# Back-to-back layer 0 projections, an on-chip transpose, LN2 behind the last adds, and pooling in pieces

## The chip, the cores and the metric

The kernel runs on the 8 cores of one Trainium2 chip (trn2). Each core computes one batch element of 8, with its own weights in its own transfers; nothing is exchanged between cores. The metric is the time of the slowest core, in microseconds (us) on the device, as the median of several executions.

In fast runs all eight cores show about the same mean granted TensorE clock (about 0.97 in the kernel before). In slow runs the cores of one die or of both show a lower clock and the time is 3 to 20% longer. Slow runs are left out everywhere below. A core here is a pipeline of TensorE (PE in the profile), VectorE (DVE), ScalarE (ACT), GpSimd (POOL) and SyncE (SP); POOL issues the DMA transfers that cast float32 to bfloat16 on the way (queue q0), SP the plain ones (queue q1).

## The reference, cut to what matters

```python
D_MODEL, BATCH, SEQ, DEPTH = 1024, 8, 2048, 4      # D_FF = 2816
for i in range(DEPTH):
    if i % 2 == 0:   # layers 0 and 2
        h = x @ w_in + b_in                        # 1024 -> 2048
        h = val * sigmoid(gate)                    # the two halves of h
        h = causal depthwise conv(h, width 31) + b_dw
        mix = silu(layer_norm(h)) @ w_out + b_out
    else:            # layers 1 and 3
        # trailing means over 2, 4, 8 and 16 tokens, one window per 256 channels,
        # minus x, then a 256x256 map per group
        mix = multiscale_pool(x, ...)
    x = layer_norm(alpha * x + mix)                # LN1
    x = layer_norm(alpha * x + swiglu(x))          # LN2
```

Most of the arithmetic is the SwiGLU feed-forward network (FFN). Softer spots are the serial chains: projection, convolution, LayerNorm, output projection, LN1, and only then the FFN.

## The kernel before

A core's 2048 tokens are two blocks of 1024, and a block is 8 "rows" of 128 tokens. The program is one list of operations with declared reads and writes; a list scheduler places them at build time, and each engine runs its own list in order. While the FFN of one block runs on TensorE, the mixer of the next stage (the other block, or the next layer) runs beside it. Only the first mixer, of block 0 in layer 0, has no FFN to hide behind.

The start loads x twice for each block, as it is and transposed on the host, and loads both blocks and the first FFN weights as soon as their buffers are free:

```python
def load_block(b):
    for i in range(4):
        plload(xTb[b][:, 2 * i:2 * i + 2]..., xt_d[b, 2 * i:2 * i + 2]..., ...)   # casting queue
    for q in range(P):
        spload(xtok[b][:, q, :], x_d[...][:, q, :], [("X", b, q)], ...)           # plain queue

load_block(0)
load_consts()
mixer(0, 0)
load_block(1)
for i, (L, b) in enumerate(stages):
    if i + 1 < len(stages):
        mixer(b2, L2)
    S.cls = 1
    ffn(b, L)
    S.cls = 0
```

The input projection takes its weights in 8 chunks through two small buffers; each chunk's result goes to a scratch tensor in memory (`scr`) and comes back in another layout as the input U of the convolution:

```python
for c in range(8):
    wo = YX_O + (c % 2) * 4 * KB
    plload(ar16(wo, 2048), win_d[L][c], ...)       # 512 KB written per chunk
    for h in range(2):                             # half the rows
        # 2 x 8 matmuls of 512 columns, two ACT evictions, one DVE product
    # store to scr[c], load scr[c] into U
for cg in range(16):
    # DVE builds masks (0.82 us each, 2 per group), 20 small matmuls, DVE adds bias
```

At the end of each FFN the sum is added row by row from PSUM and LN2 follows after every fourth row, in the same VectorE list:

```python
for q in range(P):
    # 14 or 16 matmuls for row q into one of two pairs of PSUM banks
    S.op("dve", ... xs = xs + ps ...)              # frees the pair of banks
    if last:
        ln_stats(0, xs, xk, q)
        if q % 4 == 3:
            ln_rstd(0, q - 3, q + 1)
            for qq in range(q - 3, q + 1):
                ln_apply(0, ...)                   # 2 x 1.28 us per row
```

The pooling mixer adds whole shifted copies of x: one VectorE addition covers up to 20 rows of 256 channels (5120 columns, 5.48 us in the profile). For block 0 two more passes over 2048 columns make the mean and subtract x, 2.28 us each; for block 1 one pass does both.

Of the kernel before, what the change touches and what calls it, by code (L numbers as in the profile page):

```python
# [14 lines left out]
DEPTH = 4  # L15
# [34 lines left out]
class Sched:  # L50
# [3 lines left out]
    DMA_RATE = 280e3  # L54
# [3 lines left out]
    def __init__(self):  # L58
        self.prog = []
        self.ops = {e: [] for e in self.ENGS}  # L60
        self.cnt = {e: 0 for e in self.ENGS}
        self.dcnt = {}
        self.last_w = {}
        self.readers = {}
        self.seen = {e: {} for e in self.ENGS}
        self.semkeys = set(self.ENGS)
        self.eng_free = {e: 0.0 for e in self.ENGS}
        self.dma_free = 0.0
        self.fin = {}
        self.cls = 0  # L70

    def op(self, eng, fn, reads=(), writes=(), dma=None, dur=0.5, nbytes=0, pri=0):
        self.prog.append((eng, fn, tuple(reads), tuple(writes), dma, dur, nbytes, pri + self.cls))

    def schedule(self):
        prog = self.prog
        n = len(prog)
        last_w, readers = {}, {}
        preds = [None] * n
        succs = [[] for _ in range(n)]  # L80
        for i, (eng, fn, reads, writes, dma, dur, nb, pri) in enumerate(prog):
            ps = set()
            for r in reads:
                w = last_w.get(r)
                if w is not None:
                    ps.add(w)
            for k in writes:
                w = last_w.get(k)
                if w is not None:
                    ps.add(w)  # L90
                ps.update(readers.get(k, ()))
            for r in reads:
                readers.setdefault(r, []).append(i)
            for k in writes:
                last_w[k] = i
                readers[k] = []
            ps.discard(i)
            preds[i] = ps
            for p in ps:
                succs[p].append(i)  # L100
        left = [len(p) for p in preds]
        avail = [0.0] * n
        ready = {i for i in range(n) if left[i] == 0}
        while ready:
# [14 lines left out]
            f = self.commit(prog[i], st)  # L119
# [10 lines left out]
    def commit(self, desc, start):  # L130
        eng, fn, reads, writes, dma, dur, nbytes, pri = desc
# [3 lines left out]
        else:  # L135
            self.eng_free[eng] = start + dur
            t0 = max(start + dur, self.dma_free)
            self.dma_free = t0 + nbytes / self.DMA_RATE
            fin = self.dma_free + self.DMA_LAT
        idx = len(self.ops[eng])  # L140
        deps = []
        for r in reads:
            if r in self.last_w:
                deps.append((self.last_w[r], True))
        for w in writes:
            if w in self.last_w:
                deps.append((self.last_w[w], False))
            deps.extend((t, False) for t in self.readers.get(w, ()))
        need = {}
        for (sk, val, peng, pdma), raw in deps:  # L150
            if (not pdma) and peng == eng and dma is None:
                if eng == "pe":
                    continue
# [15 lines left out]
        for r in reads:  # L169
            self.readers.setdefault(r, []).append(tick)  # L170
        for w in writes:
            self.last_w[w] = tick
            self.readers[w] = []
# [3 lines left out]
    def final_wait(self, eng, keys):  # L177
        need = {}
        for k in keys:
            t = self.last_w.get(k)  # L180
            cands = list(self.readers.get(k, ()))
            if t is not None:
                cands.append(t)
            for (sk, val, *_r) in cands:
                if need.get(sk, 0) < val:
                    need[sk] = val
# [3 lines left out]
def build():  # L190
# [6 lines left out]
    xt_d = dram("xt", [NBLK, P, 128, 8 * 128])  # L197
# [17 lines left out]
    with es:  # L215
# [56 lines left out]
        def spload(out, src, keys, sem, nbytes, reads=()):  # L272
            S.op("sp", lambda e: e.dma_start(out=out, in_=src), reads=reads, writes=keys,
                 dma=sem, dur=0.1, nbytes=nbytes)

        def plload(out, src, keys, sem, nbytes, pri=0):
            S.op("pool", lambda e: e.dma_start(out=out, in_=src), writes=keys, dma=sem,  # L277
                 dur=0.9, nbytes=nbytes, pri=pri)
# [5 lines left out]
        def ln_stats(st, src, keys, q):  # L284
            for eh in range(2):
                S.op("dve", lambda e, eh=eh: e.bn_stats(  # L286
                    out=stt[:, st, q, eh, :], in_=src[:, eh * 512:(eh + 1) * 512]),
                    reads=keys, writes=[("STT", st, q, eh)], dur=t_dve(512))
# [32 lines left out]
        def x_to_xT(b, q, slot, bank):  # L321
            S.op("act", lambda e: e.activation(out=xb[:, slot, :], in_=xtok[b][:, q, :], func=AF.Copy),  # L322
                 reads=[("X", b, q)], writes=[("XB", slot)], dur=t_act(1024))
# [17 lines left out]
        def conv_mixer(b, L):  # L341
            U_O, US_O, WC_O, WT_O, YX_O, BD_O = 0, 33 * 512, 41 * 512, 51 * 512, 61 * 512, LN1O
# [6 lines left out]
            spload(ar32(BD_O, 1024), vec_d[L, 0], ark(BD_O, 4096), "d_bd", 512e3)  # L349
            plload(ar16(WC_O, NG * ND * P), wcol_d[L], ark(WC_O, NG * ND * P * 2), "d_wc", 1.3e6)  # L350
# [6 lines left out]
            for c in range(8):  # L357
                ws = c % 2
                wo = YX_O + ws * 4 * KB
                plload(ar16(wo, 2048), win_d[L][c], ark(wo, 4096), f"d_win{ws}", 1e6)  # L360
                w = ar16(wo, 2048)
                us = c % 2
                uo = US_O + us * 2 * KB
                for h in range(2):
                    b0 = PS_M[ring("pm", 3)]
                    b1 = PS_M[ring("pm", 3)]
                    vo = YX_O + 8 * KB + ring("vb", 2) * 2 * KB
                    to = YX_O + 12 * KB + ring("th", 2) * 2 * KB

                    def mm(e, off, bank, w=w, h=h):  # L370
                        ins = None
                        for k in range(8):
                            ins = e.matmul(ps[:, bank, :], w[:, off + k * 128: off + (k + 1) * 128],
                                           xTb[b][:, 4 * h:4 * h + 4, k, :],
                                           start=(k == 0), stop=(k == 7))
                        return ins
                    rk = ark(wo, 4096) + xtk(b, range(4 * h, 4 * h + 4))
                    S.op("pe", lambda e, mm=mm, b0=b0: mm(e, 0, b0), reads=rk, writes=[("PS", b0)],
                         dur=8 * PE512)
                    S.op("pe", lambda e, mm=mm, b1=b1: mm(e, 1024, b1), reads=rk, writes=[("PS", b1)],  # L380
                         dur=8 * PE512)
                    S.op("act", lambda e, b0=b0, vo=vo, c=c: e.activation(  # L382
                        out=ar32(vo, 512), in_=ps[:, b0, :], func=AF.Identity,
                        bias=hbt[L][:, c:c + 1], scale=0.5),
                        reads=[("PS", b0), ("HB", L)], writes=ark(vo, 2048), dur=t_act(512) + 0.09)
                    S.op("act", lambda e, b1=b1, to=to, c=c: e.activation(  # L386
                        out=ar32(to, 512), in_=ps[:, b1, :], func=AF.Tanh,
                        bias=hbt[L][:, 8 + c:9 + c], scale=0.5),
                        reads=[("PS", b1), ("HB", L)], writes=ark(to, 2048), dur=t_act(512) + 0.09)
                    S.op("dve", lambda e, vo=vo, to=to, uo=uo, h=h: e.scalar_tensor_tensor(  # L390
# [484 lines left out]
```

## Time and profile before

| | before |
|---|---|
| median of fast runs | 2587.11 us (four runs, 2586.47 to 2589.12) |
| profiled execution, slowest core | 2589.9 us |
| TensorE busy | 2364.6 us, 91% |
| VectorE busy | 1612.7 us, 62% |

First the page of the kernel before: busy times, then four rows that cut the span into 40 equal slices of 65 us (digits are tenths), then the chain of work that ended last.

```profile
PE 2364.6 (91%) x12672; PEld 1146.4 (44%) x12672; DVE 1612.7 (62%) x1950; ACT 652.4 (25%) x852; POOL 229.5 (9%) x434
...
PE   2273899999999999999999999999999999999996
...
PEclk9597899999999999999999999999999999999998
DMA  9851274653764466546465276625653565347431
...
PE 78%; DVE 9%; DMA 5%; issue 5%; another core or an unknown queue 2%; POOL 1%; ACT 0%; DVEq 0%; SPq 0%; POOLq 0%; ACTq 0%
```

TensorE is full from the sixth slice on. The first five, up to 325 us, are poor, and DMA is 80% full or more in just the first two. The timeline of TensorE for the first 135 us of before (start, duration, operation, what it wrote and read, how many instructions, and in brackets the idle time ahead and what ended it) shows why:

```profile
44.41 16.87 PE L746 MATMUL ps<-sb_xT,sb_arena 128*128 128x512 bf16 x64 [44.41 <-DMA sb_arena<-win]
113.95 21.43 PE L746 MATMUL ps<-sb_xT,sb_arena 128*128 128x512 bf16 x88 [52.66 <-DMA sb_arena<-win]
```

The first matmul waits 44.4 us for the first weights, and after 64 matmuls, two chunks, TensorE stands 52.7 us for the third. In stretches of 20 us (columns: busy time of PE, PEld, DVE, ACT, POOL, then granted clock, DMA share, GB/s) the DMA engines are full with other data meanwhile, the clock falls to half, and around 210 us VectorE is full while TensorE has nothing else to do:

```profile
80.00:100.00 20.00, 0.00 (x0) 0.00 (x0) 0.00 (x0) 0.00 (x0) 0.00 (x0) 0.50 1.01 176
...
200.00:220.00 20.00, 2.60 (x12) 1.35 (x13) 20.00 (x35) 4.83 (x6) 0.00 (x0) 0.51 0.28 76
```

The first FFN matmul comes at 264.56 us:

```profile
264.56 3.59 PE L746 MATMUL ps<-sb_xT,sb_wgu 128*128 128x512 bf16 x8 [1.11 <-ACT sb_xT L318]
```

The second loss is at each FFN's end. The groups of TensorE instructions of before (count, busy us, mean ns of one, and idle ahead of them by releaser) give its sum, and the timeline its form:

```profile
L746 PE MATMUL ps<-sb_wd,sb_hT 128*128 128x512 bf16 x2816 | 637.3, 386 | 36.8 <-DVE sb_xtok L689 36.8
```

```profile
629.51 3.19 PE L746 MATMUL ps<-sb_wd,sb_hT 128*128 128x512 bf16 x14 [1.37 <-DVE sb_xtok L689]
636.74 4.88 PE L746 MATMUL ps<-sb_wd,sb_hT 128*128 128x512 bf16 x14 [4.03 <-DVE sb_xtok L689]
```

The matmuls of a row cannot start until the addition two rows earlier (line 689) has emptied their banks, and that addition stood behind this VectorE run of four LN2 operations:

```profile
630.10 4.86 DVE L306 SCALAR_TENSOR_TENSOR sb_xtok<-sb_xtok,sb_rs,sb_ln2p 128x1024 f32<-128x1024 f32 x4
```

After the wait the clock is down (0.72 on average from 636 to 642 us, 1.00 in the 6 us before) and 14 matmuls take 4.88 us, not 3.19.

### The profile page before, as it was taken

To read this page: it belongs to the slowest core of one execution; us is meant where nothing else is said; L and a number is where in the kernel's file an instruction comes from. 1 tells how busy PE (TensorE), PEld (TensorE's weight loads), DVE (VectorE), ACT (ScalarE), POOL (GpSimd) and SP (SyncE) were. 2 spreads that over 40 slices of the span, in tenths; PEclk is the share of its full clock that TensorE was granted. 3 is DMA by queue.
4 is the path that set the end of the run, shared out by engine and by line. 5 is a ranking of instruction groups with operands and counts; after the bars stand their busy time and mean duration, and the time that the engine had idled before them with its cause. 6 is when DMAs were issued, how large, how long until landed. Compare 5 with 4: busy or idle time off the path is not lost.

```text
span 2589.9 us, 31036 instructions; the slowest of 8 cores (2575.8 to 2589.9 us)
## 1 busy us (share of the span) xinstructions
PE 2364.6 (91%) x12672; PEld 1146.4 (44%) x12672; DVE 1612.7 (62%) x1950; ACT 652.4 (25%) x852; POOL 229.5 (9%) x434
## 2 busy tenths in 40 slices
PE   2273899999999999999999999999999999999996
PEld 1141345444445445544544445544445544544442
DVE  0059426868796778561686634776797679754226
ACT  1023430332113313333033342233102311322110
POOL 2000000100010001100011010100010011001100
PEclk9597899999999999999999999999999999999998
DMA  9851274653764466546465276625653565347431
GB/s 210 158 103 33 44 138 78 110 94 59 137 123 73 70 138 99 96 78 126 78 106 88 57 130 117 108 62 98 121 100 73 95 130 90 50 77 159 80 63 65
DMA packets 128566, 253.33 MB, mean 98 GB/s; under 512 B 43494, under 2 KB 56740, under 8 KB 127908
## 3 DMA queue, kind: packets, MB, share of 16 engines
q0 software_dynamic: 62944, 170.49, 42.2%
q1 hardware_dynamic: 65480, 80.85, 10.5%
q8 instruction: 101, 1.65, 0.3%
q14 instruction: 41, 0.34, 0.1%
HBM read 391.35 MB, written 16.91 MB: 158 GB/s over the span
## 4 chain that ended last, share of the span: by engine, by line
PE 78%; DVE 9%; DMA 5%; issue 5%; another core or an unknown queue 2%; POOL 1%; ACT 0%; DVEq 0%; SPq 0%; POOLq 0%; ACTq 0%
PE ps L746 76%; DMA sb_arena<-win 3%; PE ps L752 2%; DVE sb_xtok L303 2%; DVE sb_xtok L306 2%; DVE sb_stt L286 2%; DVE sb_xtok L689 1%; DMA sb_arena<-sb_xtok 1%; DMA sb_wgu<-wgu 1%; DVE sb_arena L430 0%; POOL sb_wd L277 0%; DVE sb_arena L458 0%; DMA scr_0<-sb_arena 0%; DVE sb_mv L289 0%
## 5 line engine op out<-in xcount | busy, mean ns | idle before, releaser
L746 PE MATMUL ps<-sb_xT,sb_wgu 128*128 128x512 bf16 x5632 | 1247.9, 380 | 6.3 <-DVE sb_hT L658 3.8
L746 PEld LDWEIGHTS ps<-sb_xT,sb_wgu 128*128 128x128 bf16 x5632 | 545.6, 98 | 641.6 <-DVE sb_hT L658 7.1
L746 PE MATMUL ps<-sb_wd,sb_hT 128*128 128x512 bf16 x2816 | 637.3, 386 | 36.8 <-DVE sb_xtok L689 36.8
L658 DVE TENSOR_TENSOR sb_hT<-ps,sb_sgt 128x512 bf16<-128x512 f32 x352 | 240.9, 689 | 431.2 <-PE ps L746 427.4
L654 ACT ACTIVATE sb_sgt<-ps 128x512 f32<-128x512 f32 x352 | 208.5, 597 | 1021.4 <-PE ps L746 915.6
L746 PEld LDWEIGHTS ps<-sb_wd,sb_hT 128*128 128x128 bf16 x2816 | 276.0, 99 | 372.7 <-DVE sb_xtok L689 44.2
L746 PE MATMUL ps<-sb_xT,sb_arena 128*128 128x512 bf16 x1024 | 232.2, 387 | 103.8 <-DMA sb_arena<-win 101.6
L689 DVE TENSOR_TENSOR sb_xtok<-sb_xtok,ps 128x1024 f32<-128x1024 f32 x128 | 155.8, 1217 | 94.7 <-PE ps L746 94.7
L746 PEld LDWEIGHTS ps<-sb_xT,sb_arena 128*128 128x128 bf16 x1024 | 101.0, 99 | 231.6 <-issue 111.7
L390 DVE SCALAR_TENSOR_TENSOR sb_arena<-sb_arena 128x512 bf16<-128x512 f32 x64 | 44.2, 691 | 254.3 <-ACT sb_arena L386 236.8
L277 POOL DMA_DIRECT2D sb_wgu<-wgu x176 | 93.7, 532 | 1121.6 <-PE ps L746 1093.4
L746 PE MATMUL ps<-sb_arena 128*128 128x128 bf16 (+2 forms) x1792 | 178.1, 252 | 13.2 <-DVE sb_arena L430 13.1
L286 DVE BATCH_NORM_STATS2 sb_stt<-sb_xtok 128x6 f32<-128x512 f32 x256 | 166.7, 683 | 0.8
L746 PEld LDWEIGHTS ps<-sb_arena 128*128 128x128 bf16 x1792 | 128.4, 99 | 70.0 <-DVE sb_arena L430 17.0
L277 POOL DMA_DIRECT2D sb_wd<-wd x176 | 93.8, 555 | 569.1 <-PE ps L746 503.3
L318 ACT ACTIVATE sb_xT<-ps 128x1024 bf16<-128x1024 bf16 x96 | 98.1, 1022 | 143.3 <-PE ps L752 143.1
L430 DVE TENSOR_TENSOR sb_arena<-sb_maskb,sb_arena 128x1280 bf16<-128x1280 bf16 x128 | 99.6, 816 | 43.5 <-DMA sb_arena<-wcol 33.9
L685 DVE SCALAR_TENSOR_TENSOR sb_xtok<-sb_xtok,ps 128x1024 f32<-128x1024 f32 x64 | 77.8, 1215 | 47.6 <-PE ps L746 47.5
L322 ACT ACTIVATE sb_xb<-sb_xtok 128x1024 bf16<-128x1024 f32 x80 | 84.2, 1053 | 45.6 <-DVE sb_xtok L306 45.6
L382 ACT ACTIVATE sb_arena<-ps,sb_hb 128x512 f32<-128x512 f32 x64 | 44.0, 687 | 153.8 <-PE ps L746 153.1
L303 DVE SCALAR_TENSOR_TENSOR sb_xtok<-sb_xtok,sb_mv,sb_arena 128x1024 f32<-128x1024 f32 x64 | 81.7, 1276 | 0.8
L577 DVE TENSOR_TENSOR sb_arena<-sb_arena 128x2048 f32<-128x2048 f32 (+3 forms) x24 | 80.2, 3340 | 0.0
(58 smaller groups left out, 1279.5 us busy)
## 6 DMA issues: line engine op xcount, KB each, us to landing
sb_wgu<-wgu POOLq DMA_DIRECT2D x176, 512.0 KB, 6.3
sb_wd<-wd POOLq DMA_DIRECT2D x176, 256.0 KB, 9.9
sb_arena<-win POOLq DMA_DIRECT2D x32, 512.0 KB, 7.6
sb_arena<-vec SPq DMA_DIRECT2D x24, 512.0 KB, 4.7
sb_xtok<-x SPq DMA_DIRECT2D x16, 512.0 KB, 33.1
sb_arena<-lnp SPq DMA_DIRECT2D x16, 512.0 KB, 5.5
sb_ln2p<-lnp SPq DMA_DIRECT2D x16, 512.0 KB, 9.8
sb_arena<-wout POOLq DMA_DIRECT2D x32, 256.0 KB, 4.0
```

The lines of the kernel that those rows point to most:

```text
L277: S.op("pool", lambda e: e.dma_start(out=out, in_=src), writes=keys, dma=sem, dur=0.9, nbytes=nbytes, pri=pri)
L286: S.op("dve", lambda e, eh=eh: e.bn_stats(out=stt[:, st, q, eh, :], in_=src[:, eh * 512:(eh + 1) * 512]), reads=keys, writes=[("STT", st, ...
L303: S.op("dve", lambda e: e.scalar_tensor_tensor(out=src, in0=src, scalar=mv[:, st, q, 0:1], in1=g, op0=ALU.subtract, op1=ALU.mult), reads=k ...
L318: S.op("act", lambda e: e.activation(out=dst, in_=psb[bank], func=AF.Copy), reads=[("PS", bank)], writes=dkeys, dur=t_act(1024))
L322: S.op("act", lambda e: e.activation(out=xb[:, slot, :], in_=xtok[b][:, q, :], func=AF.Copy), reads=[("X", b, q)], writes=[("XB", slot)], ...
L430: S.op("dve", lambda e, wt=wt, g0=g0: e.tensor_tensor(out=ar16(wt, 1280).rearrange("p (a c q) -> p a c q", a=10, q=P), in0=maskb[:].rearra ...
L577: S.op("dve", lambda e, B=B, nn=nn, step=step: e.tensor_tensor(out=B[:, 0:nn, :], in0=B[:, step:step + nn, :], in1=B[:, 0:nn, :], op=ALU.add),
L654: S.op("act", lambda e, h=h, bank=bank: e.activation(out=sgt[:, h, :], in_=ps[:, bank, :], func=AF.Silu), reads=[("PS", bank)], writes=[(" ...
L658: S.op("dve", lambda e, h=h, bank=bank, jj=jj: e.tensor_tensor(out=hT[:, jj, h * 512:(h + 1) * 512], in0=ps[:, bank, :], in1=sgt[:, h, :], ...
L685: S.op("dve", lambda e, xs=xs, pv=pv: e.scalar_tensor_tensor(out=xs, in0=xs, scalar=ALPHA, in1=pv, op0=ALU.mult, op1=ALU.add), reads=xk + ...
L689: S.op("dve", lambda e, xs=xs, pv=pv: e.tensor_tensor(out=xs, in0=xs, in1=pv, op=ALU.add), reads=xk + [("PS", bp), ("PS", bp + 1)], writes ...
L746: r = self.e.matmul(*a, **k)
```

## The change

The intent, in four parts:

1. **Front.** Host-transposed x is dropped; x is cast and transposed on the chip. The 8 weight chunks of layer 0 stay resident in buffers that the FFN does not need yet, so that the projections of *both* blocks use one load and block 1's projections can fill holes of block 0's chain. Block 1's x waits for block 0's scratch stores, and the early FFN weights cannot load because their buffers hold projection weights and convolution results.
2. **LN2 behind the last adds.** All eight additions of the last group come first; LN2 follows under the next stage's FFN. Only the very last FFN keeps LN2 between, in ranges of 4, 2, 1 and 1 rows.
3. **Pooling in pieces** of at most 1024 columns, one full pass less for block 0, and halo copies that may run side by side.
4. **The last FFN** takes its groups in the reverse order, so that its last group is the longest.

The diff also changes the build-time scheduler (its model of the DMA queues, and writes to one buffer that may run side by side) and lets block 0's first convolution start group by group.

The core of the diff (cut):

```diff
+        def win_home(L, c):
+            ...
+            if c < 4:
+                return (hTf[:, c * 2048:(c + 1) * 2048], [("HT", j, h) ...])
+            i = c - 4
+            return wdf[:, i * 2048:(i + 1) * 2048], [("WD", 2 * i), ("WD", 2 * i + 1)]
...
+        def first_xT(b, qs):
+            for q in qs:
+                i = 1 if b else q % 2
+                x_to_xT(b, q, i, 6 + i, cast="act" if b else "dve")
...
+        def load_x(b, qs):
             for q in range(P):
+                hold = [("SCR", 0, 0, q)] if b else []
                 spload(xtok[b][:, q, :], ..., hold)
...
-        load_block(0)
         load_consts()
+        load_x(0, range(P))
+        for c in range(8):
+            load_win(0, c)
+            if c == 1:
+                load_dw(0)
+        first_xT(0, range(P))
         mixer(0, 0)
-        load_block(1)
+        load_x(1, range(P))
+        S.cls = 1
+        first_xT(1, range(P))
+        for c in range(8):
+            p1_chunk(1, 0, c)
+        S.cls = 0
...
                     if last:
                         ln_stats(0, xs, xk, q)
-                        if q % 4 == 3:
-                            ln_rstd(0, q - 3, q + 1)
-                            for qq in range(q - 3, q + 1):
-                                ln_apply(0, ...)
+                        if end and q + 1 in (4, 6, 7, 8):
+                            ln2_tail(b, L, {4: 0, 6: 4, 7: 6, 8: 7}[q + 1], q + 1)
+                if last and not end:
+                    S.cls = 0
+                    ln2_tail(b, L, 0, 4)
+                    ln2_tail(b, L, 4, 8)
...
+        def pieces(n, m=4):
+            k = (n + m - 1) // m
+            return [(n * i // k, n * (i + 1) // k) for i in range(k)]
...
-                if nh > 1:
-                    S.op("dve", ... out=B[:, 0:nh - 1, :], in0=B[:, 1:nh, :], in1=B[:, 0:nh - 1, :] ...)
+                for a, z in pieces(nh - 1):
+                    S.op("dve", ... out=B[:, a:z, :], in0=B[:, a + 1:z + 1, :], in1=B[:, a:z, :] ...)
```

## The prediction

> **What bounds the kernel now.** TensorE is busy 91% of a 2589.9 us span (busy table). A warm 512-column matmul takes 0.2157 us (16 in 3.45 us in the timeline), a 128-column transpose about 0.055, a convolution matmul 0.065, a 256-column one 0.11. For 9984 + 1152 + 1280 + 256 of them I estimate 2332 us of pure matmul time. About 258 us are lost; the windows show where:
> - First 360 us: about 172 us of warm work, 187 us lost. The first matmul waits until 44.4 us for weights; after 64 matmuls it stands 52.7 us for weight chunk 2 (chain of waits). DMA is full until about 110 us: both blocks' x, transposed x and FFN weights, wanted only at 265 us, are ahead of those chunks. From 160 to 265 us VectorE is nearly full (convolution masks, LayerNorm) and TensorE has nothing else to do. The clock falls to 0.5 to 0.7 in the holes.
> - Seven FFN ends: 1.37 + 4.03 us idle, because two PSUM adds stand behind LN2 applies (one run of 4.86 us). The matmuls after are cold (14 take 4.7 us, not 3.05). About 7.2 us each, 50 in all.
> - The end: 15.7 us after the last matmul, about 7 before it.
> Between, TensorE has no gap worth naming, apart from 3 us behind a 5.48 us pooling add.
>
> **What the change does.**
> 1. Front. The transposed x goes away, the second block's x waits for the first block's scratch stores, FFN weights cannot be loaded early (their buffers hold other things). The first projections wait for block 0's x (4.2 MB, plain queue) and weight chunk 0. Before, about 5.7 MB plain and 3.3 MB casting transfers landed in 42 us; at these shares row 7 of x lands at about 33 us, chunk 0 at 12, and later chunks keep ahead. Projections begin at about 20 us on half the rows and run freely from 36. Added: 16 groups of 8 transposes, 7 us of TensorE; 8 casts on VectorE, 8 on ScalarE.
> The second block's projections (55 us of TensorE) fill the VectorE-bound stretch of block 0. Work before the first FFN matmul is then about 165 us, FFN start at 205 to 215 us (265 before, with the 55 us still to do). Loss in the front about 48 us instead of 187: gain 139, less 7 for transposes.
> 2. LN2 behind the last adds: an add and its statistics take 2.7 us of VectorE, one per 3.03 us of matmuls, so the adds keep up. The LayerNorm, about 20 us, moves under the next FFN, where VectorE has room; mixers end 23 us or more before they are needed. Gain about 45 of 50.
> 3. Pooling in pieces: about 3 us.
> 4. Last FFN with groups reversed: about 3 us; its tail stays VectorE-bound.
>
> Sum: 2332 + 7 + 48 + 20 (end) + 3 = 2410 us.
>
> **Prediction.** 2410 us, range 2385 to 2445. Faster by over 2%: 0.97; within 2%: 0.02; slower: 0.01.
>
> **What would show it.** First projection at 18 to 25 us, no wait for projection weights over 5 us; DMA not full at 100 us; first FFN matmul at 195 to 220 us; no wait on last FFN adds over 1 us except in the last FFN; TensorE idle behind VectorE near zero after 360 us.
>
> **What would make it wrong.** Scratch round trips stalling the in-order TensorE queue; late FFN weights; convolution and LayerNorm of block 0 stretched by block 1's work on VectorE; LN2 applies delaying FFN products in the next stage.

## The result, and the profile after

| | before | after |
|---|---|---|
| median | 2587.11 us | 2444.92 us of the three fast runs (2444.61 to 2445.84) |
| ratio of fast runs | 1 | 0.945, 95% interval 0.9431 to 0.9468 |
| profiled execution, slowest core | 2589.9 us | 2442.9 us |
| TensorE busy | 91% | 96% |
| VectorE busy | 62% | 67% |

A ratio is the mean time of one kernel's fast runs over the mean of the other's of the same rounds, so it is not quite the ratio of the medians quoted beside it. With the one slow run counted, the median of the four runs after is 2445.38 us. The output was correct. The change is faster by 142 us. The prediction was 2410 with a range of 2385 to 2445: the class is right, the number about 35 us too low, at the very edge of the range.

The page of after, the rows that answer to those above:

```profile
PE 2348.7 (96%) x12800; PEld 1152.6 (47%) x12800; DVE 1631.6 (67%) x2056; ACT 676.3 (28%) x878; POOL 219.1 (9%) x418
...
PE   4997899999999999999999999999999999999996
...
PEclk9998899999999999999999999999999999999998
DMA  8564655446744664565735464743754384428531
...
PE 89%; DMA 5%; DVE 3%; SPq 1%; issue 1%; ACT 1%; DVEq 0%; ACTq 0%
```

The first five slices are fuller (4 9 9 7 8 against 2 2 7 3 8), and VectorE's share of the chain falls from 9% to 3%. The timeline of TensorE after shows the new start:

```profile
11.04 1.03 PE L840 MATMUL ps<-sb_identb,sb_xb 128*128 128x128 bf16 x8 [11.04 <-DVE sb_xb L320]
...
28.93 3.60 PE L834 MATMUL ps<-sb_xT,sb_hT 128*128 128x512 bf16 x8 [1.12 <-ACT sb_xT L312]
...
46.91 1.03 PE L840 MATMUL ps<-sb_identb,sb_xb 128*128 128x128 bf16 x8 [3.79 <-DVE sb_xb L320]
47.74 22.24 PE L834 MATMUL ps<-sb_xT,sb_hT 128*128 128x512 bf16 x96
```

The 52.7 us wait for weights is gone. What remains is x: its rows land one by one until 46 us (the last cast, on VectorE, waits for its row), and free projections begin at 47.74, not at 36 as predicted:

```profile
46.16 0.69 DVE L320 CAST sb_xb<-sb_xtok 128x1024 bf16<-128x1024 f32 x1 [3.53 <-DMA sb_xtok<-x]
```

In front of the first FFN, and again in front of the second half of its rows, the same timeline has two holes that the prediction did not cost:

```profile
194.71 3.62 PE L834 MATMUL ps<-sb_arena,sb_wgu 128*128 128x512 bf16 x16
207.56 1.03 PE L840 MATMUL ps<-sb_identb,sb_xb 128*128 128x128 bf16 x8 [9.24 <-ACT sb_xb L317]
210.66 1.03 PE L840 MATMUL ps<-sb_identb,sb_xb 128*128 128x128 bf16 x8 [2.06 <-ACT sb_xb L317]
...
219.08 3.57 PE L834 MATMUL ps<-sb_xT,sb_wgu 128*128 128x512 bf16 x8 [1.21 <-ACT sb_xT L312]
...
247.71 3.62 PE L834 MATMUL ps<-sb_arena 128*128 128x512 bf16 x16
255.95 2.32 PE L834 MATMUL ps<-sb_arena 128*128 128x128 bf16 x20 [4.62 <-DMA sb_arena<-scr_1]
...
268.96 3.55 PE L834 MATMUL ps<-sb_xT,sb_wgu 128*128 128x512 bf16 x8 [1.12 <-ACT sb_xT L312]
```

From the output projection of row 3 (ending at 198.3) to the first FFN matmul (219.08), TensorE does four groups of 8 transposes. Each row costs 3.1 us there: a ScalarE cast, 8 transposes, a ScalarE copy, in a line; in the code all rows go through one cast buffer and one bank. The first 8 us of the hole are row 3's LN1 and the last applies on VectorE: the first cast starts at 206.45. Block 1's projections, meant as the filler, were used up just before. The same happens for rows 4 to 7 from 251.3 to 268.96. The wait of 4.62 us for scr_1 in there is not what holds it up: the first cast of that group could not start before 256.92, when VectorE's LN1 let go of its row.

LN2's waits are gone. The group of after that answers to the 36.8 us of before:

```profile
L834 PE MATMUL ps<-sb_wd,sb_hT 128*128 128x512 bf16 x2816 | 618.4, 379 | 0.9 <-DVE sb_hT L737 0.9
```

36.8 us of waiting and 18.9 us of cold matmuls (637.3 less 618.4) have become 0.9. The sum of waits of TensorE from 360 to 2424 us (us in total, times, longest), before and after:

```profile
PE ps L746 <- DVE sb_xtok L689: 31.4, 14, 4.0
PE ps L752 <- ACT sb_xb L322: 4.1, 2, 2.1
PE ps L746 <- DVE sb_hT L658: 3.8, 4, 2.5
...
```

```profile
PE ps L834 <- DVE sb_hT L737: 8.3, 6, 3.1
```

So 8.3 us of waiting for FFN products (line 737) are left, against 3.8 before. The timeline of VectorE after at one of them shows what stands in front:

```profile
585.42 2.22 DVE L620 TENSOR_TENSOR sb_arena<-sb_arena 128x768 f32<-128x768 f32 x2 [6.84 <-DMA sb_arena<-sb_xtok]
...
588.85 0.68 DVE L737 TENSOR_TENSOR sb_hT<-ps,sb_sgt 128x512 bf16<-128x512 f32 x1
```

VectorE runs in order. It stands 6.84 us at a pooling addition that waits for its halo copy, while an FFN product that could run stands behind it. The two longest waits of TensorE (2.37 us at 834.81 and 3.12 us at 1760.62) have the same form, behind halo waits of 8.52 and 9.28 us.

A tally of after, from these lines, against a pure matmul time of 2324 us (an estimate: 9984 matmuls of 512 columns at 0.2157, 1280 transposes and 1280 convolution matmuls at 0.0555 each, since 20 of the latter take 1.11 us back to back, 256 of 256 columns at 0.11):

| loss in after | us | read from |
|---|---|---|
| until 47.74 us | 41 | 47.7 less 7.0 of matmuls done |
| 48 to 194 us | 4 | small gaps at 109 to 119, cold matmuls |
| 198.3 to 219.08, and cold after | 22 | 20.7 less 1.8 of transposes, plus 2.6 |
| 251.3 to 268.96, and cold after | 17 | 17.6 less 2.9 of work, plus 2 |
| pooling waits, and cold after | 12 | 8.3, plus 1.7 twice |
| after the last matmul (2423.8) | 19 | 2442.9 less 2423.8 |
| sum | 115 | 2442.9 less 2324 is 119 |

The front of after thus loses 84 us, where 48 were predicted.

### The profile page after: what moved, and what is told of

It reads as the page before. It is cut to its first block, busy times and chain, and to the rows that moved or that the text cites. A ratio compares the mean times of both kernels' runs of the same rounds, so it can differ in the third digit from the quotient of the medians.

```text
span 2442.9 us, 31400 instructions; the slowest of 8 cores (2435.8 to 2442.9 us)
## 1 busy us (share of the span) xinstructions
PE 2348.7 (96%) x12800; PEld 1152.6 (47%) x12800; DVE 1631.6 (67%) x2056; ACT 676.3 (28%) x878; POOL 219.1 (9%) x418
## 4 chain that ended last, share of the span: by engine, by line
PE 89%; DMA 5%; DVE 3%; SPq 1%; issue 1%; ACT 1%; DVEq 0%; ACTq 0%
PE ps L834 86%; PE ps L840 3%; DMA sb_arena<-sb_xtok 2%; DMA sb_arena<-vec 2%; DVE sb_xtok L300 1%; SPq L615 1%; DVE sb_xtok L297 1%; ACT sb_xb L317 0%; DVE sb_stt L280 0%; DVE sb_hT L737 0%; DVE sb_arena L636 0%; SPq L267 0%; DVE sb_arena L620 0%; DVE sb_xtok L769 0%; DMA sb_arena<-scr_0 0%
## 5 line engine op out<-in xcount | busy, mean ns | idle before, releaser
L834 PE MATMUL ps<-sb_wd,sb_hT 128*128 128x512 bf16 x2816 | 618.4, 379 | 0.9 <-DVE sb_hT L737 0.9
L312 ACT ACTIVATE sb_xT<-ps 128x1024 bf16<-128x1024 bf16 x108 | 110.4, 1022 | 174.8 <-PE ps L840 174.8
L840 PE MATMUL ps<-sb_identb,sb_xb 128*128 128x128 bf16 x768 | 64.4, 232 | 57.5 <-DVE sb_xb L320 33.8
L834 PE MATMUL ps<-sb_xT,sb_arena 128*128 128x512 bf16 x512 | 112.8, 379 | 0.0
L462 DVE TENSOR_TENSOR sb_arena<-sb_maskb,sb_arena 128x1280 bf16<-128x1280 bf16 x128 | 100.8, 816 | 17.4 <-PE ps L834 17.4
L317 ACT ACTIVATE sb_xb<-sb_xtok 128x1024 bf16<-128x1024 f32 x88 | 92.7, 1053 | 58.5 <-DVE sb_xtok L300 55.3
L840 PEld LDWEIGHTS ps<-sb_identb,sb_xb 128*128 128x128 bf16 x768 | 53.8, 104 | 79.2 <-DVE sb_xb L320 35.5
L636 DVE TENSOR_TENSOR sb_arena<-sb_arena 128x1024 f32<-128x1024 f32 x72 | 86.2, 1213 | 0.0
L408 DVE SCALAR_TENSOR_TENSOR sb_arena<-sb_arena 128x512 bf16<-128x512 f32 x32 | 22.1, 692 | 91.0 <-ACT sb_arena L404 83.3
```

Of the source, the lines that this page charges most:

```text
L312: S.op("act", lambda e: e.activation(out=dst, in_=psb[bank], func=AF.Copy), reads=[("PS", bank)], writes=dkeys, dur=t_act(1024))
L317: S.op("act", lambda e: e.activation(out=xb[:, slot, :], in_=xtok[b][:, q, :], func=AF.Copy), reads=[("X", b, q)], writes=[("XB", slot)], ...
L462: S.op("dve", lambda e, wt=wt, g0=g0: e.tensor_tensor(out=ar16(wt, 1280).rearrange("p (a c q) -> p a c q", a=10, q=P), in0=maskb[:].rearra ...
L636: S.op("dve", lambda e, B=B, step=step, a=a, z=z: e.tensor_tensor(out=B[:, a:z, :], in0=B[:, a + step:z + step, :], in1=B[:, a:z, :], op=A ...
L834: r = self.e.matmul(*a, **k)
L840: r = self.e.transpose(*a, **k)
```

## The experiments

My theory after the result: the front is right in mechanism and short by some 36 us, because x lands late (it shares the DMA engines with the weights) and because the LN1 chain of one row after another has no filler left; LN2 paid in full; pooling in pieces matters more than I had said. The rivals were that the front's gain is mere transfer order (then holding back loads in the kernel before gives most of it), that LN2's gain comes alone, and that the late x is a share of bytes and not of packets.

The runs were made on four chips. The kernel before took means of 2584.2, 2590.7, 2588.5 and 2587.6 us on them, so differences of a few us are read as "saved against before on the same chip". After itself saves 142.3 so (0.945, interval about plus or minus 5 us).

### a_ln2_back: LN2 back among the last adds

```diff
-                if last and not end:
-                    S.cls = 0
-                    ln2_tail(b, L, 0, 4)
-                    ln2_tail(b, L, 4, 8)
+                        if not end and q % 4 == 3:
+                            ln2_tail(b, L, q - 3, q + 1)
```

> The changed kernel with one part undone: the seven inner LN2 tails stand again among the last adds, as before the change. Theory (adds behind LN2 applies): the gaps before the last adds come back, 1.4 + 4.0 us each plus cold matmuls, so 45 to 55 us slower than the changed kernel, about 2495 us. Rival (the gain at the FFN ends is small because the LayerNorm only moves and is paid again in the next FFN): under 25 us slower.

Measured: 2493.83 and 2494.61 us in its two fast runs of four, 49 us above after (saved 90.0 against before, so 52 less than after). The group of its last FFN matmuls:

```profile
L832 PE MATMUL ps<-sb_wd,sb_hT 128*128 128x512 bf16 x2816 | 637.5, 386 | 31.5 <-DVE sb_xtok L769 31.5
```

31.5 of waiting and 19.1 of cold matmuls make 50.6 us, less after's 0.9. In the new kernel LN2's place is worth about 50 us, as expected.

### e_before_ln2: the kernel before with that one part alone

```diff
-                        if q % 4 == 3:
-                            ln_rstd(0, q - 3, q + 1)
-                            for qq in range(q - 3, q + 1):
+                    if last and q == P - 1:
+                        end = (L, b) == (DEPTH - 1, NBLK - 1)
+                        S.cls = 1 if end else 0
+                        for hq in (3, 7):
+                            ln_rstd(0, hq - 3, hq + 1)
+                            for qq in range(hq - 3, hq + 1):
```

> The kernel before with one part of the change alone: LN2 behind the last adds in every FFN, pooling whole, front as before. If the parts simply add, it gains the 49 us that undoing this part cost in the changed kernel: about 2538 us. Theory (LN2 pushed into the next stage delays the pooling inputs, and whole pooling adds then hold up FFN products; in the changed kernel without pieces such waits came to 19 us instead of 8): the gaps at the FFN ends are gone, but waits behind VectorE in the pooling layers rise from 4 to 12 us or more, and the time is 2543 to 2556 us.

Measured: one fast run, 2565.36 us, 25 below before on that chip. Both expectations missed. The FFN ends are free of waits all the same; the time comes back elsewhere. The groups of e_before_ln2 (from 370 us to its last matmul) and of before (from 370 us to its last), for the last FFN matmuls and for the transposes at a mixer's end:

```profile
L749 PE MATMUL ps<-sb_wd,sb_hT 128*128 128x512 bf16 x2816 | 620.3, 379 | 5.5 <-DVE sb_xtok L685 4.1 <-DVE sb_hT L658 1.3
...
L755 PE MATMUL ps<-sb_identb,sb_xb 128*128 128x128 bf16 x576 | 46.1, 225 | 13.6 <-ACT sb_xb L322 13.6
```

```profile
L752 PE MATMUL ps<-sb_identb,sb_xb 128*128 128x128 bf16 x576 | 44.0, 219 | 4.1 <-ACT sb_xb L322 4.1
```

FFN ends give 48 us. Of these 11.6 return as waits and cold clock at mixer ends: the pooling mixer of block 0 now begins later by an LN2 and ends at 898 us, when its FFN is already waiting (its last transposes were at 863 before). About 5 return in the FFN's first matmuls, and 7 in a tail of 23 us behind the last matmul where before had 16. That leaves about 24, which agrees with the 25 measured. So LN2's 50 us need the lighter pooling and the new end; m_no_front below, which has both on the old front, waits only 4.1 us at mixer ends, as before did. One fast run carries the time; the accounting is from its profile.

### b_pool_whole: after, pooling in whole tiles

```diff
-        def pieces(n, m=4):
+        def pieces(n, m=64):
```

> The changed kernel with every pooling add whole again (pieces of up to 64 rows of the list, so one piece). The changed kernel shows four to six waits on FFN products in the two pooling layers, about 8 us idle. Theory A (these come from VectorE standing in order behind halo transfers, with LN2 now ahead of them, not from the pieces): the waits stay or grow, and the time rises by 2 to 8 us. Theory B (pieces caused them: more instructions, finer waits in the queue): the waits shrink and the time falls by 5 us or more.

Measured: one fast run, 2455.18 us; saved 129, so 10 to 13 less than after. Its groups of FFN matmuls:

```profile
L834 PE MATMUL ps<-sb_xT,sb_wgu 128*128 128x512 bf16 x5632 | 1253.2, 380 | 13.1 <-DVE sb_hT L737 10.8 <-ACT sb_xT L312 2.3
L834 PE MATMUL ps<-sb_wd,sb_hT 128*128 128x512 bf16 x2816 | 619.8, 379 | 8.4 <-DVE sb_xtok L765 6.6 <-DVE sb_hT L737 1.8
```

The waits behind VectorE outside the front are 19 us (10.8, 6.6 and 1.8), against 8.3 after. That is theory A's direction and above its 2 to 8 us. The cut of the additions is worth about 10 us, and more than the 3 predicted. That it is more because LN2 now stands in the same VectorE list at the same time is likely and not shown: no run has whole pooling and the old place of LN2 in the new kernel. One fast run carries the time.

### m_no_front: the front of before, all the rest of the change

The kernel before with after's scheduler classes, pooling mixer, FFN and LN2, but with its own loads, projections and convolution mixer (a diff of some 230 lines).

> The change without its front: the old loads, the old first layer, but LN2 behind the last adds, pooling in pieces with side by side halo transfers and the small first-block multiply, the reversed last FFN. If the parts add: undoing LN2 cost 49 us and whole pooling 10, but in the kernel before whole pooling waited only 3 to 4 us, so LN2, pooling and end are worth 50 to 57 us here, and the time is 2530 to 2540 us. LN2 alone in the kernel before brought only about 25 us because the pooling mixer then ended too late for the next FFN (two waits of 9 us); if that is due to its long chain of halo transfers and whole adds, these waits are gone here. If LN2 alone is what makes the mixer late, they stay and the time is above 2555 us.

Measured: 2544.55, 2545.64, 2549.06 us; ratio 0.9838 (0.9819 to 0.9857), saved 42. It lies some 6 us above the upper end of what was expected and below the rival. In its profile the FFN ends are free (2.1 us of waits from 370 us on) and 18.9 us follow the last matmul (15.7 in before). Its waits for weights are those of before:

```profile
L757 PE MATMUL ps<-sb_xT,sb_arena 128*128 128x512 bf16 x1024 | 233.5, 388 | 101.5 <-DMA sb_arena<-win 98.9 <-DVE sb_arena L349 1.6 <-ACT sb_arena L381 0.9
```

So the change splits into 42 us for LN2, pooling and end together, and about 100 us for the front (142 less 42).

### f_before_order and f2_before_order_late: before, with loads held back

Both hold the FFN weights of the first 9 steps and block 1's x and transposed x back, f until the sixth scratch store of block 0, f2 until the convolution's whole input has come back (`"UH"` in place of the scratch key).

```diff
+        def held(b, L, j):
+            return [("SCR", 0, 0, 5)] if (b, L) == (0, 0) and j < 9 else []
...
+                    plload(rwgu[:, sa, :], ..., reads=held(b, L, j))
...
         def load_block(b):
+            hold = [("SCR", 0, 0, 5)] if b else []
```

> The kernel before with only the order of its first transfers changed: FFN weights of the first nine steps and everything of block 1 (x and transposed x) wait for block 0's sixth scratch store. Theory (most of the front's gain is that loads not yet needed no longer stand ahead of the projection weights): the wait of 52.7 us for weight chunk 2 falls under 5 us, the first FFN matmul comes 45 to 65 us sooner, time 2520 to 2545 us. Rival (the gain comes from doing both blocks' projections back to back): little change, above 2570 us, because VectorE still holds up block 0.

> The kernel before, with FFN weights of the first nine steps and everything of block 1 held until block 0's convolution input is complete, later than in the run that held them until the sixth scratch store. There the wait for weight chunk 2 went, but the held loads, all let go at once, held up the scratch round trips (25.5 us in one wait) and the gain was 28 us. Theory (that burst ate the rest): no wait over 5 us in projections or convolution of block 0, first FFN matmul at 205 to 222 us instead of 265, time 2533 to 2552 us. Rival (block 0 is bound by VectorE, order of transfers is worth no more than the 28 us): 2555 us or more.

Measured: f 2563.06, 2560.73, 2565.58, 2560.66 (ratio 0.9891, 0.9876 to 0.9907); f2 2560.83, 2557.52, 2560.27 (0.9886, 0.9862 to 0.991). Both save 28 to 29 us and miss their expected ranges on the slow side; f2 took the time that its rival gave (2555 us or more), and f lies between its two expectations. The wait of 52.7 us is down to about 1 us in f, but the released loads meet the next transfer that the chain needs. The timeline of f, then of f2:

```profile
159.45 2.29 PE L750 MATMUL ps<-sb_arena 128*128 128x128 bf16 x20 [25.50 <-DMA sb_arena<-scr]
```

```profile
168.52 1.01 PE L756 MATMUL ps<-sb_identb,sb_xT 128*128 128x128 bf16 x8 [23.09 <-DVE sb_xT L306]
192.03 6.15 PE L750 MATMUL ps<-sb_arena,sb_xT 128*128 128x512 bf16 x15 [22.50 <-DMA sb_arena<-wout]
```

In f a scratch round trip waits 25.5 us; in f2 the weights of the output projection come 22.5 us late, after a wait of 23.1 us for VectorE. So VectorE's chain does bind block 0 there, as the rival said, but a transfer binds it as well. The first FFN matmul starts at 238 us in both (264.56 before), with block 1's projections still to do under the FFN. Order alone, as far as these two ways of holding go, gives 28 of the front's 100 us. They do not prove that no better order exists.

### c_x_first: after, weights 1 to 7 behind the rows of x

```diff
-            plload(w, win_d[L][c], k, f"d_win{c if L == 0 else c % 2}", 1e6)
+            plload(w, win_d[L][c], k, f"d_win{c if L == 0 else c % 2}", 1e6,
+                   [("X", 0, min(4 + c, 7))] if L == 0 and c else [])
...
-                load_dw(0)
+                load_dw(0, [("X", 0, 7)])
```

> The changed kernel, but weight chunks 1 and later and the convolution table wait until rows 5 to 7 of x have landed. Theory (x of block 0 lands at 46 us because half of the DMA time goes to weights that are not needed yet): x is complete at 20 to 28 us, the projections run freely from about 30 us instead of 47.7, and the time falls by 12 to 20 us. Rival (x is limited by memory or by its own queue, all eight cores loading at once): x still lands after 38 us and the time stays within 5 us or rises, since weights come later.

Measured: 2437.13, 2435.47, 2434.24, 2436.51 us; ratio 0.9426 (0.941 to 0.9442), saved 148.4, so 6 more than after (9 by the medians). The expected 12 to 20 missed. The timeline of TensorE in c:

```profile
33.17 17.44 PE L835 MATMUL ps<-sb_xT,sb_hT 128*128 128x512 bf16 x80 [1.12 <-ACT sb_xT L312]
58.37 1.23 PE L835 MATMUL ps<-sb_arena 128*128 128x128 bf16 x10 [7.76 <-DMA sb_arena<-scr]
```

The last row of x is cast at 30.70 without a wait for its transfer, and projections run freely from 33.17, 14.6 us earlier, about where the prediction had it (36). Half of that is lost 17 us later, when a convolution matmul waits for its scratch round trip. In c the DMA engines are full from 40 to 58 us and the casting queue, which holds the delayed weights, has 83.1% of their time; the scratch store and the load took 10.8 and 10.3 us from issue to landing. In after, from 50 to 70 us, the casting queue has 17.4%, and they took 3.5 and 4.6 us. The first FFN matmul comes 8.8 us earlier (210.28).

### g_win_narrow: after, each weight chunk in two transfers of half the width

```diff
+            if L == 0:
+                for i in range(2):
+                    plload(w[:, i * 1024:(i + 1) * 1024], win_d[L][c][:, i * 1024:(i + 1) * 1024],
+                           k[len(k) // 2 * i:len(k) // 2 * (i + 1)], f"d_win{c}_{i}", 0.5e6)
...
```

> The changed kernel, but each layer 0 input weight chunk is loaded by two transfers of half width (2 KB written per partition instead of 4). Same bytes, same order. Theory (the queues take turns packet by packet, so the size of the weight packets decides what share x gets): x lands at 32 to 38 us instead of 46, projections run freely from 34 to 40 us, time 5 to 12 us less. Rival (the queues share by bytes or by time): x lands at 44 to 48 us, time within 2 us.

Measured: 2436.46 and 2440.92 us in two fast runs of five; 10 more saved than after on its chip, 6 by the medians. Bytes and order are unchanged; only the packets of the casting queue are smaller. The two queues in the first 60 us, after and g (packets, MB, share of the 16 engines' time):

```profile
q0 software_dynamic: 1728, 5.18, 52.6%
q1 hardware_dynamic: 2016, 5.80, 36.7%
```

```profile
q0 software_dynamic: 2813, 5.06, 58.7%
q1 hardware_dynamic: 2247, 6.23, 36.9%
```

The packets of q0 shrink from 3.0 to 1.8 KB on average (MB over packets), the plain queue that carries x moves 6.23 MB and not 5.80, and the last row of x is cast at 39.38 us, not at 46.16. Up to 39 us, while both kernels still wait for x, the plain queue has moved 4.60 MB in g and 3.68 in after, the casting queue 2.51 and 3.36. Free projections begin at 40.96. If the queues shared by bytes, halving the packets would have changed nothing. The Trainium skill's page "DMA: Bandwidth & Descriptors", section "Queues, rings and completion order", says that each DMA engine takes turns between the queue rows at packet granularity; this run agrees: the queue with the smaller packets gave way to its neighbour. (g also makes 16 transfers instead of 8; that their number plays no part was not tested.) It also shows where my 33 us came from. I had read the plain queue's share off the first 42 us of before. There the casting packets averaged 2.0 KB (3.27 MB in 1632) and the plain queue moved 5.11 MB; in the first 39 us of after they averaged 2.9 KB (3.36 MB in 1147) and it moved 3.68.

### d_ln1_dve_cast and i_fill: after, the first hole

d puts the cast of block 0's LN1 tail in layer 0 on VectorE; i makes the last two projection chunks of block 1 wait for the LN1 statistics of row 2, so that they are left over for the hole.

```diff
-            x_to_xT(b, q, 0, 6)
+            x_to_xT(b, q, 0, 6, cast="dve" if early else "act")
```

```diff
                 rk = wk + xtk(b, range(4 * h, 4 * h + 4))
+                if (L, b) == (0, 1) and c >= 6:
+                    rk = rk + [("MV", 1, 2)]
```

> The changed kernel, but in block 0 of layer 0 the cast to bf16 ahead of the LN1 transposes runs on VectorE, not on ScalarE. TensorE order is unchanged. Theory (the two TensorE holes at 198 to 219 us and 251 to 269 us are a serial chain of cast, transposes and copy, 3.1 us for each of four rows, the cast and the copy on one engine): the step per row falls to about 2.2 us, the holes shrink by 3 to 4 us each, the time by 5 to 9 us. Rival (the holes end with something else, FFN weights or VectorE): no change over 2 us.

> The changed kernel, but the last two projection chunks of block 1 (64 matmuls, 13.8 us) wait for the LN1 statistics of row 2 of block 0, so that they run in the hole before the first FFN matmul instead of before it. Theory (the hole exists because the filler is used up too early): out-projections of rows 0 to 3 come about 6.3 us apart instead of 7.35, the hole of 19 us shrinks below 8, the first FFN matmul comes 3 to 8 us sooner, time 3 to 8 us less. Rival (the chain through VectorE has its length whatever TensorE does, and TensorE idles between the out-projections instead): time within 2 us.

Measured: d 2439.88, 2440.23, 2437.18 us (ratio 0.9439, 0.942 to 0.9457); i 2439.75, 2438.86 and 2457.68 us (0.9439, 0.9395 to 0.9484; in the third run two cores of one die had a clock of 0.979 and 0.978, and it is still called fast). By medians both are about 5 us below after, by ratio 3; the intervals overlap after's, so the times alone do not show a gain. The profiles are plainer than the times. In d a row costs 2.2 us and not 3.1, and the first FFN matmul comes at 215.86; in i the first part of the hole is filled:

```profile
189.24 13.99 PE L836 MATMUL ps<-sb_xT,sb_wd 128*128 128x512 bf16 x64
203.23 0.62 PE L842 MATMUL ps<-sb_identb,sb_xb 128*128 128x128 bf16 x8
```

and the first FFN matmul comes at 213.92. The other part, 10 us in which four rows are cast, transposed and copied, stays open (i was expected to bring the hole under 8 us), and some of what the moved filler had covered opens again: four waits of 0.87 to 1.40 us between the output projections before 189 us. The cast itself took 0.69 us on VectorE and 1.05 on ScalarE. The skill's page "VectorE: DVE Perf Modes", section "The perf-mode tier table", gives a float32 `tensor_copy` twice the rate of an operation with two tensor operands; the trace agrees, with 0.69 us for 1024 columns against 1.28 for an LN2 operation of the same size.

### k_combo and p_three: edits together

k has x first (chunks 4 to 7 paced by the scratch stores), d, i, and LN1 of rows 4 to 7 in pairs. p has g, d and i, nothing held back and no pairs: it takes away the two things that I blamed for k.

```diff
+            if L == 0 and c:
+                hold = [("X", 0, 3 + c)] if c < 4 else [("SCR", 0, 0, c - 4)]
...
-                if q % 4 == 3:
+                n = 2 if early and q > 3 else 4
+                if q % n == n - 1:
```

> The changed kernel with what the single experiments gained put together: x of block 0 first (weight chunks 1 to 3 and the convolution table wait for rows 4 to 7 of x, and new: chunks 4 to 7 are paced by the scratch stores of chunks 0 to 3, so that they don't all compete with the scratch round trip, which stalled TensorE 7.8 us when x came first), LN1 casts of block 0 on VectorE, the last two chunks of block 1 kept for the hole, and new: LN1 of rows 4 to 7 of block 0 in pairs. If the single gains (9, 5 and 6 us) add up and the pacing saves most of the stall: 2415 to 2428 us. If they overlap, because all of them only move the first FFN matmul, which one chain through VectorE decides: 2430 to 2438 us.

> The kernel after with three single edits together, none of which holds a load back and none of which reorders rows: the first projection weights in two half-width transfers (alone: about -6.5 us, free projections from 41 instead of 48), the last two projection chunks of block 1 kept for the hole in front of the first FFN (alone: about -6) and the casts of block 0's LayerNorm tail on VectorE (alone: about -5). If the combination before this one fell short because of what it added (a scratch round trip at 73 us after the holds; transposes of row pairs ahead of the last out-projections), this one shows neither stall, starts the first FFN at 202 to 208 us, ends the second hole at 252 to 258, and takes 2427 to 2434 us. Rival: the gains overlap whatever the form, because the second half-row group of the first FFN waits for the same VectorE chain: then the second hole still ends at 262 or later and the time is 2434 to 2440 us.

Measured: k 2436.03, 2440.54, 2435.97, 2436.15 us (ratio 0.9416, 0.94 to 0.9432); p 2431.71, 2433.22, 2439.5, 2438.29, 2436.4 us (0.9418, 0.9405 to 0.943). They save 151 and 152 us, 9 more than after; k's interval just touches after's, p's ends just below it. By these times they are no faster than c and g, which save 148 and 152. Neither is the sum of its parts. k still had its scratch wait, and its pairs put transposes ahead of output projections in TensorE's list. p has no such pairs, but it is not free of the scratch wait, as was expected: TensorE stands 4.01 us at 67.27. Its time fell mostly where the rival said, although its second hole ends at 260.66, between the two expectations:

```profile
72.86 2.29 PE L844 MATMUL ps<-sb_arena 128*128 128x128 bf16 x20 [9.55 <-DMA sb_arena<-scr]
...
264.50 3.59 PE L844 MATMUL ps<-sb_xT,sb_wgu 128*128 128x512 bf16 x8 [1.11 <-ACT sb_xT L312]
```

```profile
67.27 1.10 PE L841 MATMUL ps<-sb_arena 128*128 128x128 bf16 x10 [4.01 <-DMA sb_arena<-scr]
...
260.66 3.60 PE L841 MATMUL ps<-sb_xT,sb_wgu 128*128 128x512 bf16 x8 [1.11 <-ACT sb_xT L312]
```

Three marks in the timelines show where the gains go. The third is the start of the last run of 80 matmuls of the first FFN's first down-projection, which all of these kernels have in common. Each row is from the profile of one core.

| | first FFN matmul | its second half of rows | last 80 of the first down-projection |
|---|---|---|---|
| after | 219.08 | 268.96 | 339.17 |
| d | 215.86 | 263.95 | 334.65 |
| i | 213.92 | 263.69 | 334.84 |
| g | 214.38 | 265.51 | 336.38 |
| c | 210.28 | 261.53 | 332.75 |
| k | 206.63 | 264.50 | 334.83 |
| p | 212.25 | 260.66 | 331.53 |

k starts the FFN 12.5 us earlier than after and has 4.3 us left at the third mark; p starts 6.8 earlier and keeps 7.6. By these marks a front edit counts by what it does for the second half of the rows, not for the first FFN matmul. What each edit saved in all agrees with the third mark only within 7 us (g saved 10 more than after and has 2.8 at the mark).

The time of the slowest core hides part of the gain. The mean span of the eight cores over the fast runs is 153 us (k) and 154 us (p) below before on the same chip, against 148 for c and g, 147 for i and 145 for d; the cores of p lie 8.1 to 18.8 us apart within a run, those of after 4.5 to 10.7. By these means, which come from different chips, the combinations do make the cores some 5 us faster than the best single edit, and the slowest core hardly. Why their cores spread more is open.

## Why the prediction was right or wrong

The class was right: faster, by 5.5%. The number was 35 us too low. That the time still lay inside the stated range, by 0.1 us, is luck: an error of 15 us in the first term below stood against one of 36 us in the second, and without it the same argument would have given 2395. Term by term:

- **Pure matmul time, 2332 plus 7.** From the durations after it is 2324. I had put a convolution matmul at 0.065 us, and it takes 0.0555 when masks do not hold it up (12 us for 1280 of them); the rest is arithmetic, since the prediction's own durations give 2328 and not 2332. This term was 15 us too high, which hid part of the other errors.
- **Front, 48: the term that failed.** It measured 84. The mechanism held: weights resident, no wait for projection weights over 5 us, DMA at 0.66 in the stretch from 80 to 100 us, block 1's projections inside block 0's chain. The first projection came at 28.93, outside the "18 to 25" of the prediction's own signs. The size failed in three places. "Row 7 of x lands at about 33 us" measured 46, where the plain queue's share had been read from a stretch with narrower casting packets (c and g move this landing, and the start with it). "FFN start at 205 to 215 us" measured 219.08 (the signs allowed 195 to 220); of the 165 us of work that I counted ahead of it, the output projections of rows 4 to 7 (64 matmuls, 14 us) came after, so the loss up to there was larger still. And the LN1 chain had been taken as hidden, on the assertion that the second block's projections fill block 0's VectorE stretch: they ran out at 194 us, and the chain of rows 0 to 3 and again of rows 4 to 7 lay open for 22 and 17 us. d and i change the first of these holes directly.
- **LN2, 45 of 50: right.** a shows 50. What the prediction did not say is that this needs the rest: e shows that the old kernel gets 25 from it, since LN2 delays the pooling mixer.
- **Pooling in pieces, 3: too small.** b shows about 10 in the presence of LN2.
- **"TensorE idle behind VectorE near zero after 360 us": wrong.** It is 8.3 us and about 12 with the cold clock, at pooling additions that wait for halo copies in VectorE's in-order list. The list of what might go wrong had delayed FFN products in it, but behind LN2 applies; what stands ahead at the waits looked at is a pooling addition.
- **End, 20: right.** It is 19.1 us from the last matmul to the end, and no wait before it; in before it was 15.7 and about 7. The 3 at the end of the sum is not named in the prediction; if it stands for the waits between, these measured 12.
- **"Mixers end 23 us or more before they are needed": not quite, without harm.** The first pooling mixer of block 0 ends with transposes at 762.5 us, and its FFN starts at 780.48, 18 us later and without a wait.

The sum with measured terms is 2324 + 84 + 12 + 19 = 2439, against 2442.9 in the profile.

Settled: the split of about 100 us for the front and 42 for the rest, LN2's dependence on the pooling and the end (by e's profile, with one fast run), the width of the weight transfers as a lever on when x lands. Open: how much of the front's 100 us a perfect transfer order could have given in the old kernel (two tries gave 28), and why the slowest core stops near 2436 us whichever front edits are combined, while the mean of the cores still falls. The marks show gain lost between the first FFN matmul and the second half of its rows in k; in p most of it was kept.

## What to carry to other kernels

A chain of one row after another needs as much filler as it is long, at the place where it is long: count the filler to its last matmul before calling a chain hidden, and count the chain again for the second half of the rows. Holding a load back moves a wait to the next transfer that the chain needs, so look for that transfer first. A part that frees one engine early (LN2 here) should be tried together with what runs next on the engine that got the work.

## What the Trainium skill lacked or had wrong

- "TensorE: Matmul & The Clock Gate", Part 1, section "Seeing it yourself", says that a peak-current limit takes a whole die to 13/16 of the clock once three of its cores run dense matmuls, and that one should budget for that. Here all eight cores ran dense matmuls and in every fast run the granted clock was 0.97 to 0.99 on all of them (0.985 to 0.987 after). Means of 0.80 to 0.94 on the slower die occurred only in the slow runs (0.84 in the slow run after). For the fast runs the page's figure would have been about a fifth off (0.985 over 0.8125). Whether the slow runs are those in which this limit held, no run here shows; if so, the page lacks that it may hold in some executions of one program and not in others.
- The same page, Part 1, gives 215.7 ns for a warm 512-column matmul and 55.6 ns for a 128-column one, back to back, and half the clock after an idle window of about 3.4 us. The runs agree: 16 matmuls and 8 transposes from 172.65 to 176.55 us after are 3.46 and 0.44 us, and the stretch of before without a matmul had a clock of 0.50. The page says that the penalty of warming up is under 1% of a typical span; here the cold matmuls at the FFN ends cost 19 us, 0.7%, and came with waits of 1.37 and 4.03 us. So nothing is wrong in these passages.
- "DMA: Bandwidth & Descriptors" states the turn-taking by packets but not what follows for two queues that run at once: halving the transfer width of one (packets of 3.0 to 1.8 KB on average) brought the other's last row from 46.2 to 39.4 us.
- No page that I used says how late a transfer may come when many are queued ahead of it. In f a 256 KB scratch load made TensorE wait 25.5 us, where the median scratch load of the same run took 5.0 us from issue to landing.
